# 2048 rows of the FFN's second weight in seven block products, with block sums made by DMA during the mixer

## The chip, the cores and the metric

The kernel runs on one core of one Trainium2 chip. The metric is device time in microseconds (us) of one execution. The engines that matter here are PE (TensorE, matrix products), DVE (VectorE), ACT (ScalarE), POOL (GpSimd, which is nearly idle but can issue DMAs) and SP (SyncE, which issues the DMAs of the kernel before). An engine works through its own instructions in the order in which the program lists them. An instruction whose operand isn't ready holds up all that stands behind it on that engine.

## The reference, cut to what matters

Two layers, 512 tokens, width 1024, all in float32:

```python
def swiglu(u, wi, wo):
    gate, up = jnp.split(u @ wi, 2, axis=-1)
    return (jax.nn.silu(gate) * up) @ wo          # wo: 2816 x 1024

for l in range(DEPTH):                            # DEPTH = 2
    mix = hybrid_mixer(h, ...)                    # projections, attention, recurrent branch
    h = layer_norm(ALPHA * h + mix, ...)
    h = layer_norm(ALPHA * h + cross_attention(h, mem, ...), ...)
    h = layer_norm(ALPHA * h + swiglu(h, wi[l], wo[l]), ...)
```

The change concerns the last product, `(512 x 2816) @ (2816 x 1024)`, once in each layer.

## The kernel before, in words

Every product is made to float32 accuracy out of three PE matmuls: each operand is split into a high and a low part, and high x high, high x low and low x high are added up in PSUM. So a matmul pass over a pair of 128x128 and 128x512 blocks costs three instructions.

**Weights.** The class `Weights` holds a list of pages of 128x1024 in the order of their use. `dma` has SP load a page (512 KB) into one of four buffers `raw`. `split` then makes the high half on ACT (`whi<-raw`, L122) and the low half on DVE (`wlo<-raw,whi`, L123), each into a slot of a pool of 32 pages, and starts further loads. `next` hands a page out and splits ahead as far as `la` says. The 32 slots are shared with activations and LayerNorm operands: whoever takes a slot waits until the last reader of its old tile is done.

**Matmuls.** All of them are recorded by the helper `mm` (L250), so rows are told apart by tiles. `later` and `tick` put deferred work behind so many nanoseconds of counted PE work. In `norm` each token tile's transposes (`pt`, L254) are deferred in this way: by 9500 for the first three token tiles, by 8000 for the last.

**A layer** goes through `mixer` (input projections with the attention in between, then the weights of the attention branch, the recurrent branch and gates, `w_br_rnn`, `w_out`), `cross` and `ffn`. In `ffn` the first weight is multiplied in quads (`q`, `c`: tiles of 128x256, seven block products instead of eight, with sums of weight blocks made on DVE). The hidden activations `h` stand transposed, 128 of the 2816 rows to a half page.

**The second weight** (`wo`) goes through `out_norm`: 22 pages of 128 rows. For each page and each of four token tiles there are six matmuls of 128x512 into that token tile's two PSUM banks `acc`, that is 528 matmuls per layer. The split activations are `hs` (ACT L277, DVE L278). The last pages are taken token tile by token tile, and `norm` follows each of them. The FFN's input `x`, needed as the residual, is loaded back from DRAM (`x<-x_keep`) near the end of the pages.

Of the kernel before, what the change touches and what calls it, by code (L numbers as in the profile page):

```python
# [7 lines left out]
F32 = mybir.dt.float32  # L8
F32R = mybir.dt.float32r
AF = mybir.ActivationFunctionType  # L10
ALU = mybir.AluOpType
# [3 lines left out]
P = 128  # L15
S = 512
# [25 lines left out]
def f(ap):  # L42
    return ap.bitcast(F32)


class Weights:
# [27 lines left out]
    def rows(self, w, c0, n):  # L74
        for k in range(n):
            self.specs.append([(w[k * P:(k + 1) * P, c0:c0 + D], lambda t: t)])

    def gates(self, a, b):
        for n in range(4):
            self.specs.append([  # L80
                (m[n].rearrange("(k p) c -> p k c", p=P),
                 lambda t, i=i: t[:, i * 512:(i + 1) * 512].rearrange("p (k c) -> p k c", k=2))
                for i, m in enumerate((a, b))])
# [22 lines left out]
    def split(self):  # L106
        j = self.n_split
        if j >= len(self.specs):
            return
        while self.n_dma <= j:  # L110
            self.dma()
        if j in self.quad:
            self.drain()
            self.gen = self.split_quad(j)
            self.drain()
            return
        self.n_split += 1
        nc = self.K.nc
        raw = self.raw.pop(j)
        hi = self.K.page(F32R, "whi")  # L120
        lo = self.K.page(F32R, "wlo")
        nc.scalar.activation(out=hi, in_=raw, func=AF.Copy)  # L122
        nc.vector.tensor_sub(out=lo, in0=raw, in1=f(hi))  # L123
        self.parts[j] = (hi, lo)
        while self.n_dma < min(len(self.specs), j + 1 + N_RAW):
            self.dma()

# [91 lines left out]
class Trunk:  # L219
    def __init__(self, ctx, tc, a):  # L220
        self.tc = tc
        self.nc = tc.nc
        self.a = a
        self.L = a["w_in"].shape[0]
        pool = lambda name, bufs, **kw: ctx.enter_context(tc.tile_pool(name=name, bufs=bufs, **kw))
        self.const = pool("const", 1)
        self.pg = pool("pg", N_PAGES)
        self.raw = pool("raw", N_RAW)
        self.hpool = pool("hp", 8)
        self.smp = pool("sm", 3)  # L230
        self.sml = pool("sml", 8)
        self.psp = pool("ps", 8, space=PSUM)
        self.W = Weights(self)
        self.now = 0.0
        self.pend = []

    def page(self, dt=F32, name="pg"):
# [205 lines left out]
    def norm(self, t, ps, g, b, last):  # L443
# [52 lines left out]
                                               op0=ALU.mult, op1=ALU.add)  # L496
            nc.sync.dma_start(out=self.a["out"][t * P:(t + 1) * P, c], in_=xt[:, c])
        if not last:
            self.later(9500.0 if t < NT - 1 else 8000.0, lambda: self.xT_due(t))
            if self.want_T:  # L500
                nc.sync.dma_start(out=self.x_dram[t * P:(t + 1) * P, :], in_=xt)

    def out_norm(self, act, nk, res, gv, bv, last=False, prefetch=0, between=None,
                 want_T=False, restore=False, spread=0.0):
# [6 lines left out]
        acc = [[self.ps("acc") for _ in range(2)] for _ in range(NT)]  # L511
        self.x_done = [False] * NT
        self.want_T, self.spread = want_T, spread
        self.Bf = {}

        cut = last

        def step(k, t, w, parts=((0, S), (S, D))):
            ah, al = act(k)
            hi, lo = w  # L520
            cs = slice(t * P, (t + 1) * P)
            kw = {"skip_group_check": True} if parts[0][1] - parts[0][0] < S else {}
            out = lambda c0, c1: acc[t][c0 // S][:, c0 % S:c0 % S + c1 - c0]
            for c0, c1 in parts:
                self.mm(out(c0, c1), ah[:, cs], hi[:, c0:c1], k == 0, False, **kw)
# [6 lines left out]
        for k in range(nk - res):  # L532
# [158 lines left out]
    def schedule_weights(self):  # L691
        a, W = self.a, self.W
        for l in range(self.L):
# [70 lines left out]
    def mixer(self, l, params):  # L764
# [279 lines left out]
    def ffn(self, l, last):  # L1044
        nc, a, W = self.nc, self.a, self.W
        W.la = 0
        H, hs = {}, {}

        def act(m, g, u0, u1):
            s = self.half(name="silu")  # L1050
            nc.scalar.activation(out=s, in_=g, func=AF.Silu)
            if m % 2 == 0:
                pg = self.page(F32, "h")
# [21 lines left out]
        act(1, p[2], p[3], None)  # L1075
        self.xt = [None] * NT
        for m in range(2, NF):
            act(m, *self.proj_pair())
        W.la = 2
# [28 lines left out]
    def run(self):  # L1108
        nc, a = self.nc, self.a
        self.xt = [self.page(F32, "x") for _ in range(NT)]  # L1110
        self.mT_dram = [self.tc.dram_tile([P, 2, 2, MEM], F32, name="mT_keep%d" % i) for i in range(4)]
        self.x_dram = self.tc.dram_tile([S, D], F32, name="x_keep")
        self.xT = self.const.tile([P, ND, 2, S], F32R, name="xT")
        self.ident = self.const.tile([P, P], F32, name="ident")
# [76 lines left out]
```

## Time and profile before

| what | value |
|---|---|
| median of 3 runs | 1893.18 us (1892.93 to 1893.5) |
| the profiled execution, its span | 1893.48 us, 1891.7 us |
| PE busy, TensorE clock granted | 1875.8 us (99%), 0.998 |
| DVE, ACT, POOL busy | 1360.0 us (72%), 1011.3 us (53%), 27.6 us (1%) |
| DMA moved | 217.63 MB, mean 115 GB/s |

The span is the time from the first to the last instruction. The execution is 1.78 us longer than its span. Busy time counts an engine's instructions, not its waits. PE's 99% says that nearly all of the time is time in which a matmul is under way. It doesn't say that each matmul is at its shortest.

### The profile page before, as it was taken

What the parts mean: (1) busy time and instruction counts of PE and PEld (TensorE: products, weight loads), DVE (VectorE), ACT (ScalarE), POOL (GpSimd) and SP (SyncE); (2) the same over time, 40 slices, a digit from 0 to 9 for tenths busy, and PEclk for the clock granted to TensorE, in tenths of its full rate; (3) what the DMA queues carried; (4) which work ended last, traced back from release to release, by engine and by line L of the source; (5) the groups of instructions that cost most, each with busy time, mean ns of one, the idle gap of its engine ahead of it and who ended that gap; (6) DMA issues with size and microseconds to landing.
All of it is one profiled execution on the core that took longest, in us unless ns stands there. A gap on an engine that the chain in (4) does not pass through costs nothing.

```text
span 1891.7 us, 28939 instructions
## 1 busy us (share of the span) xinstructions
PE 1875.8 (99%) x11201; PEld 1665.3 (88%) x11201; DVE 1360.0 (72%) x2435; ACT 1011.3 (53%) x1989; POOL 27.6 (1%) x74
## 2 busy tenths in 40 slices
PE   9999999999999999999999999999999999999998
PEld 8888888888998999988898888888889889999886
DVE  6997367569767888873579964675688598888634
ACT  5675167336664655652346742773367565565521
POOL 0000000000000000000000000000000000000001
PEclk9999999999999999999999999999999999999999
DMA  6434133355434333354214441333652523333531
GB/s 183 112 101 119 49 98 91 101 179 176 125 124 145 90 112 102 101 190 144 67 46 104 109 123 44 101 94 96 200 171 86 177 91 101 102 109 107 187 100 45
DMA packets 277754, 217.63 MB, mean 115 GB/s; under 512 B 7793, under 2 KB 254065, under 8 KB 277617
## 3 DMA queue, kind: packets, MB, share of 16 engines
q1 hardware_dynamic: 277616, 215.79, 38.0%
q8 instruction: 88, 1.44, 0.3%
q14 instruction: 50, 0.40, 0.1%
HBM read 196.89 MB, written 12.58 MB: 111 GB/s over the span
## 4 chain that ended last, share of the span: by engine, by line
PE 95%; DVE 3%; issue 0%; DMA 0%; ACT 0%; SPq 0%; DVEq 0%
PE ps L250 39%; PE q L250 25%; PE acc L250 22%; PE cv L250 2%; PE sc L250 2%; PE av L250 1%; PE cs L250 1%; PE pT L254 1%; PE pt L254 1%; DVE wlo L123 1%; DVE Bf L355 1%; DMA raw<-in_w_in_dram 0%; PE cT L254 0%; DVE xT L275 0%; SPq L1125 0%
## 5 line engine op out<-in xcount | busy, mean ns | idle before, releaser
L250 PE MATMUL ps<-xT,whi 128*128 128x512 f32 (+1 forms) x1728 | 478.2, 365 | 0.5 <-ACT whi L102 0.5
L123 DVE TENSOR_TENSOR wlo<-raw,whi 128x1024 fp32r<-128x1024 f32 x239 | 290.7, 1222 | 146.9 <-ACT whi L122 118.0
L250 PEld LDWEIGHTS ps<-xT,whi 128*128 128x128 f32 x1728 | 297.3, 188 | 44.2 <-ACT whi L102 0.7
L122 ACT ACTIVATE whi<-raw 128x1024 fp32r<-128x1024 f32 x239 | 249.8, 1054 | 140.3 <-PE acc L250 52.4
L250 PE MATMUL ps<-xT,wlo 128*128 128x512 f32 (+1 forms) x864 | 311.3, 362 | 0.2
L250 PE MATMUL acc<-whi,hs 128*128 128x512 f32 (+1 forms) x714 | 218.3, 387 | 0.5 <-ACT hs L277 0.5
L250 PEld LDWEIGHTS ps<-xT,wlo 128*128 128x128 f32 x864 | 162.0, 188 | 28.0 <-DVE wlo L123 0.6
L250 PEld LDWEIGHTS acc<-whi,hs 128*128 128x128 f32 x714 | 133.5, 188 | 28.0 <-ACT hs L277 0.9
L250 PE MATMUL q<-xT,wq 128*128 128x256 f32 x1152 | 154.2, 281 | 0.0
L250 PEld LDWEIGHTS q<-xT,wq 128*128 128x128 f32 x1152 | 144.1, 189 | 0.2
L409 ACT ACTIVATE c<-q 128x256 f32<-128x256 f32 x192 | 73.5, 383 | 129.9 <-PE q L250 129.3
L250 PE MATMUL acc<-wlo,hs 128*128 128x512 f32 (+1 forms) x357 | 137.9, 386 | 0.0
L275 DVE TENSOR_TENSOR wql<-s,wqh 128x512 fp32r<-128x512 f32 x192 | 129.2, 685 | 1.4 <-ACT wqh L274 1.2
L274 ACT ACTIVATE wqh<-s 128x512 fp32r<-128x512 f32 x192 | 115.0, 622 | 15.7 <-DVE s L152 14.5
L275 DVE TENSOR_TENSOR wq<-raw,wq 128x512 fp32r<-128x512 f32 x144 | 98.6, 685 | 0.0
L274 ACT ACTIVATE wq<-raw 128x512 fp32r<-128x512 f32 x144 | 89.6, 622 | 1.4 <-DMA raw<-in_cq_w_dram 1.4
L250 PE MATMUL acc<-whi,mg 128*128 128x512 f32 x256 | 80.5, 392 | 0.0
L250 PE MATMUL acc<-whi,cO 128*128 128x512 f32 x256 | 79.7, 390 | 0.0
L250 PE MATMUL ps<-ya,whi 128*128 128x512 f32 x256 | 78.8, 389 | 0.0
L250 PE MATMUL ps<-yr,whi 128*128 128x512 f32 x256 | 78.8, 389 | 0.0
L250 PEld LDWEIGHTS acc<-wlo,hs 128*128 128x128 f32 x357 | 67.0, 188 | 13.4
L250 PE MATMUL q<-T4h,wq 128*128 128x256 f32 x384 | 76.6, 282 | 0.0
(233 smaller groups left out, 3974.8 us busy)
## 6 DMA issues: line engine op xcount, KB each, us to landing
raw<-in_ffn_wi_dram SPq DMA_DIRECT2D x88, 512.0 KB, 3.8
raw<-in_w_in_dram SPq DMA_DIRECT2D x84, 512.0 KB, 3.8
raw<-in_ffn_wo_dram SPq DMA_DIRECT2D x44, 512.0 KB, 4.2
raw<-in_ckv_w_dram SPq DMA_DIRECT2D x32, 512.0 KB, 4.3
raw<-in_w_br_attn_dram SPq DMA_DIRECT2D x16, 512.0 KB, 4.1
raw<-in_w_br_rnn_dram SPq DMA_DIRECT2D x16, 512.0 KB, 4.0
raw<-in_w_out_dram SPq DMA_DIRECT2D x16, 512.0 KB, 3.7
x_keep<-x SPq DMA_DIRECT2D x16, 512.0 KB, 2.6
```

Of the source, the lines that this page charges most:

```text
L122: nc.scalar.activation(out=hi, in_=raw, func=AF.Copy)
L123: nc.vector.tensor_sub(out=lo, in0=raw, in1=f(hi))
L250: self.nc.tensor.matmul(out, lhsT=lhsT, rhs=rhs, start=start, stop=stop, **kw)
L254: self.nc.tensor.transpose(out, in_, self.ident)
L274: nc.scalar.activation(out=hi, in_=src, func=AF.Copy)
L275: nc.vector.tensor_sub(out=lo, in0=src, in1=f(hi))
L355: nc.vector.tensor_tensor(out=o, in0=x, in1=y, op=ALU.subtract)
L409: cp = lambda out, in_: nc.scalar.activation(out=out, in_=in_, func=AF.Copy)
```

## The change

For rows 0 to 2047 of `wo` (16 of the 22 pages) the product of a 512x2048 and a 2048x1024 matrix is cut 2 by 2 into blocks: tokens in halves of 256, the inner dimension in halves of 1024, the columns in halves of 512. Seven products of sums of blocks take the place of eight products of blocks. A page of a weight block holds two row blocks of 128 and 512 columns, so each product has four pages with 12 matmuls each. The last six pages go through `out_norm` as before and add to the same PSUM banks (`acc=acc, k0=16`).

- The weight's block sums B11+B12, B12+B22, B11+B12+B22 and B11+B12+B22+B21 are made in DRAM (`wsum`): ten DMAs for a group of 128 rows, eight groups per layer, all issued by POOL. Two of the ten move one element of a weight's page (`whi`) and stand first, so that the group starts when that page exists. A group is issued at every fifth split page from the end of the attention on.
- The activations' block sums (`hsum`, and in place in `h`) are made on DVE and split (`hq`) in the same way as `hs`. Two operands are made during the last two quads (`ahead`).
- Four of the seven products are added into `x` by DVE (`into_x`), so `x` is now loaded ahead of the seven products. `W.la` is 3 during them.
- In `norm` the last token tile's transposes are deferred by 9000 instead of 8000, in every `out_norm` but the last.

```diff
+    def blocks(self, w):
+        for j in range(4):
+            self.specs.append([(w[j * 256:(j + 1) * 256, :].rearrange("(k p) c -> p k c", p=P),
+                                lambda t: t.rearrange("p (k c) -> p k c", k=2))])
...
         self.parts[j] = (hi, lo)
+        self.K.block_sums(hi)
...
-            self.later(9500.0 if t < NT - 1 else 8000.0, lambda: self.xT_due(t))
+            self.later(9500.0 if t < NT - 1 else 9000.0, lambda: self.xT_due(t))
...
-            W.rows(a["ffn_wo"][l], 0, NF)
+            wo, t = a["ffn_wo"][l], self.wsum[l]
+            for b in (wo[0:D, 0:S], t[0], t[1], wo[D:2 * D, 0:S], t[2], wo[D:2 * D, S:D], t[3]):
+                W.blocks(b)
+            W.rows(wo[2 * D:DFF, :], 0, NF - 2 * ND)
+
+    def block_sums(self, page):
+        self.n_page += 1
+        if not self.bg or self.n_page % 5:
+            return
+        l, j = self.bg.pop(0)
+        dma = self.nc.gpsimd.dma_start
...
+        t1, t2, t3, t4 = (t[j * P:(j + 1) * P, :] for t in self.wsum[l])
+        for t in (t1, t3):
+            dma(out=t[0:1, 0:1], in_=f(page[0:1, 0:1]))
+        for out, in_, add in ((t1, B11, 0), (t3, B12, 0), (t1, B12, 1), (t3, B22, 1),
+                              (t2, t1, 0), (t2, B22, 1), (t4, t2, 0), (t4, B21, 1)):
+            kw = {"accum_op": ALU.add} if add else {}
+            dma(out=out, in_=in_, **kw)
...
         self.tick(flush=True)
+        self.bg = [(l, j) for j in range(8)]
...
+        W.la = 3
+        self.T = {}
+        self.xt = [self.page(F32, "x") for _ in range(NT)]
+        for t in range(NT):
+            nc.sync.dma_start(out=self.xt[t], in_=self.x_dram[t * P:(t + 1) * P, :])
+        acc = seven()
...
         W.la = 2
-        self.T = {}
         self.out_norm(h_parts, NF, R3, a["ln3_g"][l], a["ln3_b"][l], last=last,
-                      prefetch=0 if last else F3, restore=True)
+                      prefetch=0 if last else F3, acc=acc, k0=2 * ND)
...
+        def product(p, b, first):
+            for j in range(4):
+                hi, lo = (t.rearrange("p (k c) -> p k c", k=2) for t in W.next())
+                i = p * 4 + j
+                while todo and todo[0][0] * 4 + todo[0][1] <= i + 2:
+                    operand(*todo.pop(0))
+                ah, al = ops.pop((p, j))
+                for k in range(2):
+                    for t in range(2):
+                        c = slice(t * P, (t + 1) * P)
+                        self.mm(b[t], ah[:, k, c], hi[:, k, :], first and j + k == 0, False, **kw)
+                        self.mm(b[t], ah[:, k, c], lo[:, k, :], False, False, **kw)
+                        self.mm(b[t], al[:, k, c], hi[:, k, :], False, j + k == 4, **kw)
+                    self.tick()
+
+        def into_x(t0, hf, b, op):
+            for t in range(2):
+                x = self.xt[t0 + t][:, hf * S:(hf + 1) * S]
+                tt(out=x, in0=x, in1=b[t], op=op)
```

On POOL, before stood 64 small copies `sm<-sk` of the attention and nothing else until the end of the last layer. Now 80 DMAs stand behind the attention's copies of each layer. This is one group of the first layer (`wsum_0` to `wsum_3` are the four sums in DRAM, `whi` the page that it waits for, DMASW the semaphores on which POOL waits for its own earlier DMAs):

```order
L752 DMA wsum_0_86<-whi 1x1 [waits Activation_49]
L752 DMA wsum_2_88<-whi 1x1
L756 DMA wsum_0_86<-in_ffn_wo_dram 128x512 [waits DMASW6_49]
L756 DMA wsum_2_88<-in_ffn_wo_dram 128x512 [waits DMASW7_49,DMASW1_49]
L756 DMA wsum_0_86<-in_ffn_wo_dram 128x512 [waits DMASW0_49]
L756 DMA wsum_2_88<-in_ffn_wo_dram 128x512 [waits DMASW1_49]
L756 DMA wsum_1_87<-wsum_0_86 16x4096 [waits DMASW2_49]
L756 DMA wsum_1_87<-in_ffn_wo_dram 128x512 [waits DMASW5_49,DMASW4_49]
L756 DMA wsum_3_89<-wsum_1_87 16x4096 [waits DMASW5_49]
L756 DMA wsum_3_89<-in_ffn_wo_dram 128x512 [waits DMASW6_49]
```

Each of these DMAs waits for the one whose result it needs, and POOL issues nothing of the next group before the last of this one is issued.

On DVE, in the stage of the `w_br_rnn` pages of the first layer, one of the eight `wlo` now waits for POOL's DMAs too (DMASW5 and DMASW4), because it takes the slot of a page that a group's one-element DMAs read. Of the changed kernel:

```order
L922 SCALAR_TENSOR_TENSOR mg<-gate,ps 128x512 [waits PE_49]
L923 TENSOR_TENSOR mg<-mg,gate 128x512 [waits DVE_49]
L287 SCALAR_TENSOR_TENSOR mg<-mg 128x512 [waits Activation_49]
L129 TENSOR_TENSOR wlo<-raw,whi 128x1024 [waits DMASW5_49,DMAHW7_49,DMASW4_49,Activation_49]
L922 SCALAR_TENSOR_TENSOR mg<-gate,ps 128x512 [waits PE_49]
```

Each group has one such first waiter, on ACT, DVE or SP. Before, no row waits for a DMASW semaphore there.

On DVE, in the stage of the second weight of the first layer, a row pair repeated before, one `hs` and one `wlo` for 24 matmuls:

```order
L278 SCALAR_TENSOR_TENSOR hs<-h,hs 128x512 x3
L123 TENSOR_TENSOR wlo<-raw,whi 128x1024
L278 SCALAR_TENSOR_TENSOR hs<-h,hs 128x512
L123 TENSOR_TENSOR wlo<-raw,whi 128x1024
L278 SCALAR_TENSOR_TENSOR hs<-h,hs 128x512
L123 TENSOR_TENSOR wlo<-raw,whi 128x1024
```

Now operand sums (L1153, L1155) and additions into `x` (L1184) stand between them, here from the end of the first product to the end of the second, and there are 12 matmuls to a `wlo`:

```order
L1153 TENSOR_TENSOR hsum<-h 128x512 x2
L1184 TENSOR_TENSOR x<-x,acc 128x512
L287 SCALAR_TENSOR_TENSOR hq<-hsum,hq 128x512
L129 TENSOR_TENSOR wlo<-raw,whi 128x1024
L287 SCALAR_TENSOR_TENSOR hq<-hsum,hq 128x512
L1184 TENSOR_TENSOR x<-x,acc 128x512
L129 TENSOR_TENSOR wlo<-raw,whi 128x1024
L1153 TENSOR_TENSOR hsum<-h 128x512 x2
L1155 TENSOR_TENSOR hsum<-hsum,h 128x512
L287 SCALAR_TENSOR_TENSOR hq<-hsum,hq 128x512
L129 TENSOR_TENSOR wlo<-raw,whi 128x1024
```

An addition into `x` waits for the last matmul of a product, and the split pages that stand behind it wait with it.

## Rows read from the trace of the kernel before

**Rows 1.** The page: busy us of each engine, and the granted clock in 40 slices.

```profile
PE 1875.8 (99%) x11201; PEld 1665.3 (88%) x11201; DVE 1360.0 (72%) x2435; ACT 1011.3 (53%) x1989; POOL 27.6 (1%) x74
...
PEclk9999999999999999999999999999999999999999
```

**Rows 2.** The chain that ended last: start us, us, what.

```profile
172.12 220.18 PE ps L250 x957
...
626.24 198.58 PE q L250 x1668
826.50 110.50 PE acc L250 x486
...
1762.77 120.18 PE acc L250 x543
```

**Rows 3.** PE's waits: what for, us in total, times, longest us.

```profile
PE pt L254 <- DVE x L488: 2.2, 4, 0.9
PE scr L1097 <- DVE idle L1089: 1.5, 1, 1.5
PE ps L250 <- DVE wlo L123: 1.5, 2, 0.7
PE acc L250 <- ACT hs L277: 0.5, 2, 0.3
```

**Rows 4.** PE's timeline, second weight: start us, us, engine, line, what.

```profile
896.94 0.84 PE L250 MATMUL acc<-whi,hs 128*128 128x512 f32 x3
897.62 0.39 PE L250 MATMUL acc<-wlo,hs 128*128 128x512 f32 x1
897.84 0.39 PE L250 MATMUL acc<-whi,hs 128*128 128x512 f32 x1
898.07 0.39 PE L250 MATMUL acc<-wlo,hs 128*128 128x512 f32 x1
898.30 0.84 PE L250 MATMUL acc<-whi,hs 128*128 128x512 f32 x3
...
902.38 0.84 PE L250 MATMUL acc<-whi,hs 128*128 128x512 f32 x3
```

**Rows 5.** Stretches: us, busy us of each engine, granted clock, DMA share, GB/s.

```profile
626.00:826.50 200.50, 200.23 (x1683) 200.03 (x1682) 167.39 (x309) 114.22 (x237) 0.00 (x0) 1.00 0.37 111
826.50:926.00 99.50, 99.50 (x439) 82.36 (x440) 42.02 (x48) 35.07 (x44) 0.00 (x0) 1.00 0.48 151
1387.00:1425.00 38.00, 37.12 (x222) 32.95 (x222) 33.31 (x48) 23.82 (x38) 0.00 (x0) 1.00 0.67 201
215.70:445.00 229.30, 229.29 (x1035) 187.94 (x1034) 147.23 (x204) 120.89 (x179) 0.00 (x0) 1.00 0.38 117
```

**Rows 6.** DVE groups of 626 to 926 us: busy us, mean ns of one.

```profile
L123 DVE TENSOR_TENSOR wlo<-raw,whi 128x1024 fp32r<-128x1024 f32 x26 | 31.8, 1223 | 40.6 <-ACT whi L122 25.4 <-issue 8.8 <-PE acc L250 6.4
L278 DVE SCALAR_TENSOR_TENSOR hs<-h,hs 128x512 fp32r<-128x512 f32 x22 | 14.9, 686 | 11.3 <-ACT hs L277 11.3
L152 DVE TENSOR_TENSOR s<-raw 128x512 f32<-128x512 f32 x18 | 12.3, 685 | 0.0
```

**Rows 7.** DVE's timeline at the end of the quads.

```profile
809.63 0.69 DVE L275 TENSOR_TENSOR wql<-s,wqh 128x512 fp32r<-128x512 f32 x1
810.24 0.69 DVE L161 TENSOR_TENSOR s<-raw,s 128x512 f32<-128x512 f32 x1
810.84 0.69 DVE L275 TENSOR_TENSOR wql<-s,wqh 128x512 fp32r<-128x512 f32 x1
```

**Rows 8.** The page, two of ACT's groups: busy us, mean ns of one.

```profile
L122 ACT ACTIVATE whi<-raw 128x1024 fp32r<-128x1024 f32 x239 | 249.8, 1054 | 140.3 <-PE acc L250 52.4
...
L274 ACT ACTIVATE wqh<-s 128x512 fp32r<-128x512 f32 x192 | 115.0, 622 | 15.7 <-DVE s L152 14.5
```

**Rows 9.** DMA issues: engine, count, KB each, median us from issue to landing.

```profile
raw<-in_ffn_wo_dram SPq DMA_DIRECT2D x44, 512.0 KB, 4.2
x_keep<-x SPq DMA_DIRECT2D x16, 512.0 KB, 2.6
Q<-Qhl SPq DMA_DIRECT2D x48, 128.0 KB, 2.3
ln_b<-in_ln_b_dram SPq DMA_DIRECT2D x6, 512.0 KB, 8.1
raw<-in_w_rg_dram SPq DMA_DIRECT2D x8, 256.0 KB, 2.7
out_dram<-y SPq DMA_DIRECT2D x8, 256.0 KB, 2.0
```

**Rows 10.** Timeline of ACT, DVE and SP behind the first layer's attention.

```profile
174.38 1.99 ACT L122 ACTIVATE whi<-raw 128x1024 fp32r<-128x1024 f32 x2
...
368.28 1.23 DVE L123 TENSOR_TENSOR wlo<-raw,whi 128x1024 fp32r<-128x1024 f32 x1 [0.26 <-ACT whi L122]
...
392.62 0.43 SPq L508 DMA_DIRECT2D ln_g<-in_ln_g_dram  x1
```

More of the change, by code (lines that the diff above doesn't have):

```diff
@@ L234, in __init__ @@
         self.now = 0.0
+        self.bg = []
+        self.n_page = 0
         self.pend = []
@@ L503, in out_norm @@
     def out_norm(self, act, nk, res, gv, bv, last=False, prefetch=0, between=None,
-                 want_T=False, restore=False, spread=0.0):
+                 want_T=False, restore=False, spread=0.0, acc=None, k0=0):
         nc = self.nc
@@ L510, in out_norm @@
         nc.sync.dma_start(out=b, in_=bv.partition_broadcast(P))
-        acc = [[self.ps("acc") for _ in range(2)] for _ in range(NT)]
+        fresh = [[acc is None or n is None for n in row] for row in acc] if acc else [[True] * 2] * NT
+        acc = [[acc[t][i] if not fresh[t][i] else self.ps("acc") for i in range(2)] for t in range(NT)]
         self.x_done = [False] * NT
@@ L521, in step @@
             cs = slice(t * P, (t + 1) * P)
-            kw = {"skip_group_check": True} if parts[0][1] - parts[0][0] < S else {}
+            kw = {"skip_group_check": True} if k0 or parts[0][1] - parts[0][0] < S else {}
             out = lambda c0, c1: acc[t][c0 // S][:, c0 % S:c0 % S + c1 - c0]
             for c0, c1 in parts:
-                self.mm(out(c0, c1), ah[:, cs], hi[:, c0:c1], k == 0, False, **kw)
+                self.mm(out(c0, c1), ah[:, cs], hi[:, c0:c1], k == k0 and fresh[t][c0 // S], False, **kw)
                 self.mm(out(c0, c1), ah[:, cs], lo[:, c0:c1], False, False, **kw)
@@ L530, in step @@
             self.tick()
-        for k in range(nk - res):
+        for k in range(k0, nk - res):
             w = self.W.next()
@@ L723, in schedule_weights @@
                 W.quads(a["ffn_wi"][l], m * P, DFF + m * P)
-            W.rows(a["ffn_wo"][l], 0, NF)
+            wo, t = a["ffn_wo"][l], self.wsum[l]
[8 more added lines that the diff above has]
+        dma = self.nc.gpsimd.dma_start
+        wo = self.a["ffn_wo"][l]
+        B11, B12, B21, B22 = (wo[r * D + j * P:r * D + (j + 1) * P, c * S:(c + 1) * S]
+                              for r in range(2) for c in range(2))
+        t1, t2, t3, t4 = (t[j * P:(j + 1) * P, :] for t in self.wsum[l])
[5 more added lines that the diff above has]
+            dma(out=out, in_=in_, **kw)
     def layer_params(self, l):
@@ L1046, in ffn @@
         W.la = 0
-        H, hs = {}, {}
+        H, Hp, hs = {}, {}, {}
         def act(m, g, u0, u1):
@@ L1052, in act @@
             if m % 2 == 0:
-                pg = self.page(F32, "h")
+                pg = Hp[m // 2] = self.page(F32, "h")
                 H[m], H[m + 1] = pg[:, :S], pg[:, S:]
@@ L1077, in ffn @@
         for m in range(2, NF):
+            if m == NF - 2:
+                seven, ahead = self.wo_seven(Hp)
+            if m >= NF - 2:
+                ahead()
             act(m, *self.proj_pair())
+        W.la = 3
[4 more added lines that the diff above has]
+        acc = seven()
+        for m in range(2 * ND):
+            H.pop(m)
+        Hp.clear()
@@ L1079, in ffn, with wo_seven, s, operand @@
         W.la = 2
-        self.T = {}
         self.out_norm(h_parts, NF, R3, a["ln3_g"][l], a["ln3_b"][l], last=last,
-                      prefetch=0 if last else F3, restore=True)
+                      prefetch=0 if last else F3, acc=acc, k0=2 * ND)
+    def wo_seven(self, Hp):
+        nc, W = self.nc, self.W
+        tt = nc.vector.tensor_tensor
+        h = lambda j, tok: Hp[j].rearrange("p (k s) -> p k s", k=2)[:, :, tok * 256:(tok + 1) * 256]
+        st, ops = {}, {}
+        def s(j):
+            if j // 2 not in st:
+                st[j // 2] = self.page(F32, "hsum")
+            return st[j // 2][:, j % 2 * S:(j % 2 + 1) * S].rearrange("p (k s) -> p k s", k=2)
+        def operand(p, j):
+            if p in (0, 3):
+                src = h(j + (4 if p else 0), 0)
+            elif p == 6:
+                src = h(j + 4, 1)
+            elif p == 4:
+                src = h(j, 0)
+                tt(out=src, in0=src, in1=h(j, 1), op=ALU.subtract)
+            else:
+                src = s(j)
+                if p == 1:
+                    tt(out=src, in0=h(j, 1), in1=h(j + 4, 1), op=ALU.subtract)
+                elif p == 2:
+                    tt(out=src, in0=src, in1=h(j, 0), op=ALU.subtract)
+                else:
+                    tt(out=src, in0=src, in1=h(j + 4, 0), op=ALU.add)
+            t = self.page(F32R, "hq")
+            hi, lo = (t[:, i * S:(i + 1) * S].rearrange("p (k s) -> p k s", k=2) for i in range(2))
+            self.split_to(hi, lo, src, scale=1.0 / ALPHA)
+            ops[p, j] = hi, lo
+        todo = [(p, j) for p in range(7) for j in range(4)]
+        def product(p, b, first):
+            kw = {} if first else {"skip_group_check": True}
+            for j in range(4):
[15 more added lines that the diff above has]
+                tt(out=x, in0=x, in1=b[t], op=op)
+        bank = lambda: [self.ps("acc") for _ in range(2)]
+        def run():
+            b1 = bank()
+            product(0, b1, True)
+            into_x(0, 0, b1, ALU.add)
+            b2 = bank()
+            product(1, b2, True)
+            into_x(2, 1, b2, ALU.add)
+            product(2, b1, False)
+            into_x(0, 1, b1, ALU.subtract)
+            b3 = bank()
+            product(3, b3, True)
+            product(4, b1, False)
+            into_x(2, 1, b1, ALU.subtract)
+            product(5, b2, False)
+            product(6, b1, False)
+            return [[b3[0], b2[0]], [b3[1], b2[1]], [b1[0], None], [b1[1], None]]
+        return run, lambda: operand(*todo.pop(0))
@@ L1111, in run @@
         self.mT_dram = [self.tc.dram_tile([P, 2, 2, MEM], F32, name="mT_keep%d" % i) for i in range(4)]
+        self.wsum = [[self.tc.dram_tile([D, S], F32, name="wsum%d_%d" % (l, i)) for i in range(4)]
+                     for l in range(self.L)]
         self.x_dram = self.tc.dram_tile([S, D], F32, name="x_keep")
```

## The prediction

> **What bounds the kernel now.** I read the page first. PE is busy 99% of the span at full granted clock, DVE 72%, ACT 53% [rows 1]. The reader is to see two things: no clock is to be won, and hardly any idle time of PE. The chain of waits says the same in order of time. It is made of long unbroken pieces of matmuls. The second weight is the piece of 110.50 us from 826.50 in the first layer and the one of 120.18 us from 1762.77 in the second [rows 2]. The list of PE's waits holds only some 6 us, of which 2.2 us, in four places, are transposes that wait for the end of LayerNorm [rows 3].
>
> Busy 99% could hide matmuls that are slower than they need be, so I read the timeline of PE in the second weight. One record is 0.39 us long because they overlap, but the starts are what counts. From 898.30 to 902.38 there are 18 matmuls in 4.08 us, so one is issued each 0.2267 us [rows 4]. This pitch holds whichever operand is used. The kernel is bound by the number of matmuls, and fewer of them is time won, as long as what feeds them keeps up. That second half decides, so I read the stretches: in this stage DVE is busy 42.02 of 99.50 us, ACT 35.07, DMA 0.48. In the quads before it DVE is at 167.39 of 200.50 us, and PE still misses only 0.27 us [rows 5].
>
> **The change, part by part.**
>
> *Matmuls.* Sixteen pages of 24 matmuls are 384 per layer. Seven products of 4 pages with 12 each are 336. So 48 fall away per layer, 96 in all, of the same 128x512 shape. 96 x 0.2267 = **-21.8 us**. This is the only large gain. It can't be larger, since PE's pitch is fixed.
>
> *Feeding the products.* A page now lasts 12 x 0.2267 = 2.72 us of PE, where it lasted 5.44, and there are 28 of them in place of 16, so 76.2 us per layer. DVE has, per page, one `wlo` (1.22 us), one `hq` like `hs` (0.69), 16/28 of an operand sum and 8/28 of an addition into `x`, both like the 128x512 sums of the quads (0.685) [rows 6]. That is 1.22 + 0.69 + 0.39 + 0.20 = 2.50 us, 92% of 2.72. Back to back the instructions overlap (in the quads they start 0.60 us apart [rows 7]), so I expect some 2.3 us, 83%, as in the quads, where PE lost next to nothing. ACT has 1.05 + 0.62 us per page [rows 8], which is less. Loads are 512 KB per 2.72 us, 193 GB/s. The stretch with the nearest load is the cross-attention's K and V (1387 to 1425): 201 GB/s, DMA share 0.67, DVE 33.31 of 38 us. There PE is idle 0.88 us of 38, 2.3% [rows 5]. Taken over to 76.2 us this is 1.8 us per layer, **+3.5 us** for both. It also stands for the start of the second product, where DVE, in its program order, waits for the last matmul of the first before it goes on to operands that PE needs soon. Bounds: 0, as in the quads, and 9 us per layer, which is worked out with the rivals.
>
> *The loads of `x` and the additions into it.* The four loads are only moved ahead on SP; `x` is first read behind a whole product of 10.9 us, and a load of this size lands in 4.2 [rows 9]. The eight additions are in DVE's 2.50 us. PE waits for one only where a product takes its bank again, and another product of 10.9 us lies between each time. **0 us**; what they may cost as a stop on DVE is in the bound of 9.
>
> *Transposes of the last token tile, 1000 ns later.* One more us of matmuls goes ahead of them. The four waits are 2.2 us together, the longest 0.9 [rows 3], so nearly all is covered: **-2.0 us**, bounds -2.2 and 0 (the work put ahead is PE work that exists anyway).
>
> *Block sums by DMA.* They cost no engine time but POOL's issuing, and POOL has nothing else to do there. They can cost in one way: the page which starts a group is held until the group's one-element DMAs have read it. These stand on POOL behind the whole group before. The next user of that slot on ACT, DVE or SP waits, and in-order work behind it too. In the first layer the page of the first group is written at 174.4. The first waiter of the seventh group is a `wlo` that DVE ran at 368.3, that of the eighth SP's `ln_g` at 392.6 [rows 10]. If a group takes C from its first DMA to the next group's, the seventh starts at 174.4 + 6C, and PE has some 6 us more before it needs that page (it is split two pages ahead). So nothing is held while 6C < 368.3 + 6 - 174.4 = 200, C < 33 us. For `ln_g`, with 7C < 218 and about 15 us of buffered loads behind it on SP, C < 33 comes out again. The sums themselves are read only in the last quads, more than 350 us later. I take the second layer as the first.
>
> C is six dependent steps: a one-element DMA, a copy, an add, a copy, an add, a copy. No row shows a DMA issued by POOL, one from DRAM to DRAM, or one that adds, so I bound it. A write of 256 KB out landed in 2.0 us, a load of 256 KB in 2.7, a store of 512 KB in 2.6 [rows 9]. Below: 2.0 + 5 x 2.7 = 15.5 us. Above: load and store one after the other, 5.3 a step, and for the two adds another 2.7 to read the target: 2.0 + 5 x 5.3 + 2 x 2.7 = 33.9. I take about 25, near the middle, since a copy reads and writes at the same time but an add reads twice. All but the very end of these bounds costs nothing: **0 us**. At 33.9 it would be 6 x 33.9 - 200 = 3 us per layer.
>
> The Trainium skill gives a price for a DMA issued from GpSimd ("DMA: Bandwidth & Descriptors", Anatomy of one DMA): about 2.0 us fixed, mostly the receipt from the target memory, plus bytes over 436 GB/s. By this an estimate of a 256 KB step is 2.6 us and of C 15 us, and nothing would be held. [...]
>
> *Sum*, against the profiled execution: 1893.48 - 21.8 + 3.5 - 2.0 + 0 = 1873.2. That execution is 0.3 above the median of the runs, which is less than I can tell. **1873 us**, 1.1% faster.
>
> **Rivals.**
>
> *A, the products are fed too slowly.* For it speaks that DVE is at 92% by plain durations and `x` additions stop it in order. Four of them with 2 x 0.69 us are 5.5 us per layer if nothing hides them. If loads landed in 8.1 us like `ln_b` [rows 9], a `raw` buffer would be taken for 8.1 + 1.05 + 1.22 + about 1 = 11.4 us, four buffers give a page per 2.84 us, 0.12 too slow, 28 times: 3.4 us. Together 9 per layer: 1873 - 3.5 + 18 = **1888 us**. Against it: `W.la = 3` splits three pages, 8.2 us, ahead, and loads of this weight land in 4.2 us [rows 9].
>
> *B, slower: the chain of block sums is longer than the pages' pace.* This is the hold above, beyond its point. From C = 35 on, 6C - 200 = 10 us per layer eat the whole gain. If each step took 8.1 us, like the longest loads [rows 9], C is 48.6, the seventh group's page is held 92 us per layer, and the time is 1873 + 184 = **2057 us**. C = 38 gives 28 per layer, 1929 us. For it: six steps in series without overlap, of a kind that no row shows, and my upper bound reaches its threshold. Against it: it needs steps of 5.8 us on average with 256 KB or less, where 512 KB loads land in 4.2.
>
> *C, the block sums slow the weight loads.* A group writes 8 x 256 KB, 2.1 MB in some 27 us, 77 GB/s next to the 117 GB/s and the DMA share of 0.38 of that stretch [rows 5]. In proportion the share becomes 0.63, or 0.88 if reading counts again. A page there lasts 5.44 us, so four buffers bear 4 x 5.44 - 3.3 = 18 us of landing time. Loads would have to become four times as slow; at 20 us a page takes (20 + 3.3) / 4 = 5.8 us, and 45 pages lose 17 us per layer: **1907 us**. The Trainium skill speaks for this rival ("DMA: Bandwidth & Descriptors", Issuing engines are not separate DMA queues): DMAs issued by GpSimd run on the same 16 engines and interleave with SP's. No row here shows two issuers at once; the K and V stretch shows only that a share of 0.67 of one queue is borne.
>
> **How the numbers follow.** My forecast 0.70, with its own range 1869 (no stall, all 2.2 us of the transposes won) to 1880 (twice the stalls, no gain from the transposes, a few held us). A 0.12, its slower half at or near no change, B 0.15, C 0.03. A measurement of this kernel can tell about 0.2%, 3.8 us. Faster: 0.70 + 0.06 = 0.76, same 0.06, slower 0.15 + 0.03 = 0.18. The range takes the forecast and A: 1868 to 1891, and leaves B and C out.
>
> **What would show it.** The second weight's piece of the chain about 11 us shorter in each layer, with matmuls still 0.227 apart. PE's waits for `wlo` or `hq` some 1 to 2 us per layer at the first and second product. The `pt` waits gone. Between 174 and 420 us and in the same stretch of the second layer, PE without gaps, and POOL's DMAs landing in about 4 us each with groups some 27 us apart. I'm wrong if ACT, DVE or SP wait there for POOL's DMAs, if landing times of `raw` pass 18 us, or if PE's waits in the products add up to more than 5 us per layer.

## The result, and the profile after

The change takes the median from 1893.33 us (1892.93 to 1893.5, 4 runs) to **1870.34 us** (1869.67 to 1870.37, 4 runs). The ratio is 0.9877, with a 95% interval of 0.9863 to 0.9892. The profiled execution of the changed kernel took 1869.67 us, its span is 1867.9 us. I had forecast 1873 us, in a range of 1868 to 1891.

The page of the changed kernel, busy us of each engine and the granted clock, answers to [rows 1]:

```profile
PE 1855.3 (99%) x11105; PEld 1648.1 (88%) x11105; DVE 1428.0 (76%) x2531; ACT 1045.7 (56%) x2037; POOL 129.9 (7%) x234
...
PEclk9999999999999999999999999999999999999999
```

PE has 96 matmuls less and is 20.5 us less busy; DVE has 68 us more to do. PE's share stays at 99%, which alone would not tell the two kernels apart.

The chain of the changed kernel in order of time (start us, us, what), at the same places as [rows 2], with the second weight's pieces at 825.19 and 1749.83:

```profile
171.75 220.20 PE ps L259 x957
...
825.19 99.84 PE acc L259 x438
925.91 5.47 PE acc L259 x24
...
1098.65 220.19 PE ps L259 x957
...
1749.83 109.56 PE acc L259 x495
```

And two more pieces of the chain of the kernel before:

```profile
937.87 5.47 PE acc L250 x24
...
1110.59 220.20 PE ps L250 x957
```

The pieces of the quads can't be compared by their starts, since they hold 1668 matmuls before and 1678 after. So these places are taken from PE's timeline, at a matmul that has the same number of matmuls ahead of it in both kernels: the first one that reads `T1h`, an operand of the quads, and the first of the second weight. In the first layer, of the kernel before and then of the change:

```profile
627.50 0.28 PE L250 MATMUL q<-T1h,wqh 128*128 128x256 f32 x1
...
826.50 0.50 PE L250 MATMUL acc<-whi,hs 128*128 128x512 f32 x1 [0.27 <-ACT hs L277]
```

```profile
626.44 0.28 PE L259 MATMUL q<-T1h,wqh 128*128 128x256 f32 x1
...
825.03 0.40 PE L259 MATMUL acc<-whi,hq 128*128 128x512 f32 x1
```

Read side by side, the starts give the gain stage by stage:

| place | before | after | gained since the place above |
|---|---|---|---|
| end of the first attention | 172.12 | 171.75 | 0.37 |
| quads of the first FFN, first `T1h` | 627.50 | 626.44 | 0.69 |
| second weight's first matmul | 826.50 | 825.03 | 0.41 |
| its last pages | 937.87 | 925.91 | 10.49 |
| second layer, behind the attention | 1110.59 | 1098.65 | -0.02 |
| quads of the second FFN, first `T1h` | 1563.77 | 1551.06 | 0.77 |
| second weight's first matmul | 1762.77 | 1749.66 | 0.40 |
| end of the span | 1891.7 | 1867.9 | 10.69 |

So 21.2 of 23.8 us come from the stage of the second weight, 1.5 from the transition into the FFN, 0.8 from the transition into the second weight, and 0.4 from the start of the program. The last is no effect of the change: in the runs below in which nothing delays it, the same piece begins anywhere from 171.70 to 172.34. The stretch that holds most of the block sums, from 172 to 392 us and again from 1099 us, is as long as before, 220.20 us.

PE's waits in the changed kernel answer to [rows 3]; neither `pt` nor `acc` stands among them now:

```profile
PE ps L259 <- DVE wlo L129: 1.8, 4, 0.7
PE scr L1220 <- DVE idle L1212: 1.5, 1, 1.5
PE ps L259 <- ACT whi L108: 0.4, 1, 0.4
```

The stretches of the seven products (all of them in the first layer, then an inner one) and the stretch behind the attention, with the columns of [rows 5]:

```profile
825.20:901.50 76.30, 76.30 (x335) 62.50 (x335) 69.91 (x88) 47.85 (x62) 0.00 (x0) 1.00 0.73 244
...
836.00:847.00 11.00, 11.00 (x48) 8.45 (x47) 11.00 (x15) 4.52 (x6) 0.00 (x0) 1.00 0.43 144
...
215.00:445.00 230.00, 229.99 (x1040) 188.61 (x1039) 147.89 (x207) 121.05 (x180) 40.27 (x62) 1.00 0.66 175
```

DVE is busy 69.91 of 76.30 us and in an inner stretch without any pause, 11.00 of 11.00. DVE is near its limit here, and one of the runs below shows how near. PE's busy time misses nothing, but it hides something: the 48 matmuls of the second product take 11.40 us in the first layer and 11.41 in the second, where 48 x 0.2267 are 10.88. PE's loads of the stationary operand, which have an engine row of their own (PEld), do wait there (us in total, times, longest):

```profile
PEld acc L259 <- DVE hq L287: 1.0, 4, 0.3
PEld acc L259 <- ACT hq L286: 0.7, 2, 0.4
```

DVE's largest group in the same stretch (x count | busy us, mean ns | idle before):

```profile
L129 DVE TENSOR_TENSOR wlo<-raw,whi 128x1024 fp32r<-128x1024 f32 x33 | 40.1, 1219 | 3.2 <-PE acc L259 2.1 <-ACT whi L128 1.1
```

In the last row of the stretches DMA works at a share of 0.66 in place of 0.38, and PE misses nothing either.

One group of block sums on POOL in the first layer, start us, us, what, with what ended the wait before it in brackets:

```profile
320.20 1.07 POOL L752 DMA_DIRECT2D wsum<-whi  x2 [2.48 <-ACT whi L128]
324.13 1.08 POOL L756 DMA_DIRECT2D wsum<-in_ffn_wo_dram  x2 [2.85 <-DMA wsum<-whi]
329.14 1.69 POOL L756 DMA_DIRECT2D wsum<-in_ffn_wo_dram  x2 [3.94 <-DMA wsum<-in_ffn_wo_dram]
335.71 0.52 POOL L756 DMA_DIRECT2D wsum<-wsum  x1 [4.87 <-DMA wsum<-in_ffn_wo_dram]
341.13 0.82 POOL L756 DMA_DIRECT2D wsum<-in_ffn_wo_dram  x1 [4.90 <-DMA wsum<-wsum]
346.16 0.52 POOL L756 DMA_DIRECT2D wsum<-wsum  x1 [4.21 <-DMA wsum<-in_ffn_wo_dram]
...
349.83 1.32 POOL L752 DMA_DIRECT2D wsum<-whi  x2
...
380.41 1.31 POOL L752 DMA_DIRECT2D wsum<-whi  x2
```

The group begins when its page is there (ACT `whi` ended the wait), takes six dependent steps, and 29.6 us later the next begins, without a wait for its page: from here on in this layer the chain sets the pace, not the pages. The next one, the eighth and last, follows 30.6 us later, and its own last DMA is issued 35.3 us after its first (415.73). In the second layer the chain sets the pace four times, with 27.2, 25.3, 27.0 and 29.9 us, and the last group takes 35.6. The order on POOL is not quite the one told ahead of the prediction: in the first layer the second group's one-element DMAs go out at 193.47, ahead of the first group's last steps, and the two groups run into each other. The landing times (KB each, median us), and what loads next to them paid:

```profile
wsum<-in_ffn_wo_dram POOLq DMA_DIRECT2D x96, 256.0 KB, 4.8
...
wsum<-wsum POOLq DMA_DIRECT2D x32, 256.0 KB, 3.6
raw<-in_w_br_rnn_dram SPq DMA_DIRECT2D x16, 512.0 KB, 6.1
...
wsum<-whi POOLq DMA_DIRECT2D x32, 0.0 KB, 3.5
```

The medians for one element, 3.5 us, and for a copy of 256 KB within DRAM, 3.6, lie close together, but they hide a wide spread. Ten of the 32 one-element DMAs landed in 1.5 to 1.6 us. The other 22 took 2.9 to 7.5, and 18 of these went out while the last add of the group before was still under way. The copies of 256 KB took 2.8 us at least. How much of a step's time goes with its bytes is not shown, since no run changed them.

### The profile page after: what moved, and what is told of

Read it like the earlier page. It is cut to its first block, busy times and chain, and to the rows that moved or that the text cites. A ratio compares the mean times of both kernels' runs of the same rounds, so it can differ in the third digit from the quotient of the medians.

```text
span 1867.9 us, 29249 instructions
## 1 busy us (share of the span) xinstructions
PE 1855.3 (99%) x11105; PEld 1648.1 (88%) x11105; DVE 1428.0 (76%) x2531; ACT 1045.7 (56%) x2037; POOL 129.9 (7%) x234
## 3 DMA queue, kind: packets, MB, share of 16 engines
q0 software_dynamic: 13824, 33.57, 8.8%
## 4 chain that ended last, share of the span: by engine, by line
PE 97%; DVE 2%; ACT 0%; issue 0%; DVEq 0%
PE ps L259 41%; PE q L259 26%; PE acc L259 21%; PE cv L259 2%; PE sc L259 2%; PE av L259 1%; PE cs L259 1%; PE pt L263 1%; PE pT L263 1%; DVE wlo L129 1%; PE cT L263 0%; DVE Bf L364 0%; DVE xT L284 0%; PE scr L1220 0%; DVE cK L284 0%
## 5 line engine op out<-in xcount | busy, mean ns | idle before, releaser
L129 DVE TENSOR_TENSOR wlo<-raw,whi 128x1024 fp32r<-128x1024 f32 x263 | 319.3, 1220 | 91.1 <-ACT whi L128 87.9
L128 ACT ACTIVATE whi<-raw 128x1024 fp32r<-128x1024 f32 x263 | 274.9, 1053 | 99.5 <-DMA raw<-in_w_out_dram 17.1
L259 PE MATMUL acc<-whi,hq 128*128 128x512 f32 x448 | 139.2, 391 | 0.0
L283 ACT ACTIVATE wqh<-s 128x512 fp32r<-128x512 f32 x192 | 115.0, 622 | 15.7 <-DVE s L159 15.5
L259 PEld LDWEIGHTS acc<-whi,hq 128*128 128x128 f32 x448 | 83.8, 188 | 18.9 <-DVE hq L287 1.0
L259 PE MATMUL acc<-wlo,hq 128*128 128x512 f32 x224 | 87.2, 389 | 0.0
L756 POOL DMA_DIRECT2D wsum<-in_ffn_wo_dram x96 | 70.2, 761 | 211.7 <-DMA wsum<-wsum 110.4
```

What stands on the lines that cost most here:

```text
L259: self.nc.tensor.matmul(out, lhsT=lhsT, rhs=rhs, start=start, stop=stop, **kw)
L283: nc.scalar.activation(out=hi, in_=src, func=AF.Copy)
L756: dma(out=out, in_=in_, **kw)
```

## The experiments

My theory: the time is matmuls times pitch, everything added hides below PE, and it stands on two things, DVE's rate in the products and the pace of the block sums' chain. The rivals: the added traffic costs something after all (so the gain could be larger without it); the hold of pages is harmless; the deeper split-ahead `W.la = 3` is what feeds the products.

### Is anything of the block sums paid for? (no_sums)

```diff
-        self.bg = [(l, j) for j in range(8)]
...
-            for b in (wo[0:D, 0:S], t[0], t[1], wo[D:2 * D, 0:S], t[2], wo[D:2 * D, S:D], t[3]):
+            for b in (wo[0:D, 0:S], wo[0:D, S:D], wo[D:2 * D, 0:S], wo[D:2 * D, 0:S], wo[0:D, S:D],
+                      wo[D:2 * D, S:D], wo[0:D, 0:S]):
```

> The changed kernel without any of the 160 block-sum DMAs: where a product should read a sum of two or more blocks of the weight, it reads one block of the weight, so the output is another one; matmuls, splits and loads are the same in number and shape. If the block sums are hidden completely (my theory), 1870.3 within 0.7 us. If their traffic or the held pages cost something that the profile does not show as a wait, it is faster by 1 us or more, and the two stretches of 220 us behind the attention become shorter.

Measured: **1870.47 us** (1870.11 to 1870.58), against 1870.34 with the sums. The stretch behind the first attention, in the run without sums, with the columns as above:

```profile
171.75:392.00 220.25, 220.25 (x960) 179.80 (x959) 128.92 (x155) 105.89 (x142) 0.00 (x0) 1.00 0.32 93
```

DMA works at half the share there, 0.32 in place of 0.65 with the sums, and PE's time is the same. So the 160 DMAs and 33.57 MB cost nothing that this comparison can tell, as they are placed.

### The transposes (last_8000, before_9000)

```diff
-            self.later(9500.0 if t < NT - 1 else 9000.0, lambda: self.xT_due(t))
+            self.later(9500.0 if t < NT - 1 else 8000.0, lambda: self.xT_due(t))
```

> The changed kernel with the last token tile's transposes deferred by 8000 again. By the two traces the later transposes gave back 0.47 us at each of the two transitions from cross-attention to FFN: 1870.3 + 0.9 = 1871.3 us, with PE's waits for x (L488's line) back at 0.9 us twice. By the sum of the prediction (2.0 us at four places): 1872.3.

Measured: **1871.61 us** (1871.08 to 1872.31), 1.3 us above the change. The wait is back in the list:

```profile
PE pt L263 <- DVE x L497: 2.2, 4, 0.9
```

The kernel before with 9000 alone:

> The kernel before with only the transposes deferred by 9000 in place of 8000. 1893.3 - 0.9 = 1892.4 us if the gain is 0.47 us at two places, 1891.3 if it is the 2.0 us of the prediction, 1893.3 if the wait only moves.

Measured: **1892.13 us** (1891.87 to 1892.38, 10 runs), where the kernel before has 1893.06 beside it (1892.81 to 1893.46, 13 runs): 0.9 us, with a ratio of 0.9995 (0.9985 to 1.0004) whose interval includes no change. So this edit alone stays within what the interval can tell; the two pairs of medians give 1.3 and 0.9 us, both less than the sum's 2.0. PE's timeline says what became of the rest. Its matmuls from the third token tile's transposes to the last one's (window, us, PE busy and its matmuls in brackets, then the columns of [rows 5]), and these transposes, of the kernel before and then of the change:

```profile
603.00:610.98 7.98, 7.08 (x62) 6.90 (x60) 7.98 (x19) 5.45 (x12) 0.00 (x0) 1.00 0.01 2
...
610.98 1.06 PE L254 MATMUL pt<-ident,x 128*128 128x128 f32 x8 [0.90 <-DVE x L488]
```

```profile
602.64:610.61 7.97, 7.90 (x69) 7.72 (x67) 7.97 (x19) 5.45 (x12) 0.00 (x0) 1.00 0.01 2
...
610.61 1.06 PE L263 MATMUL pt<-ident,x 128*128 128x128 f32 x8
```

The transposes begin as late as before (0.37 us earlier, the offset of the whole program), because the LayerNorm that they wait for ends when it did. Seven more matmuls of 0.12 us now run ahead of them, 0.83 us; 0.13 of it is lost again right behind them, and 0.70 us is won. The second layer wins the same, and so does each layer in the trace of before_9000. That is 1.4 us, at two of the four places; at the others it was 0.2 us waits that moved to the next `wlo`. The 0.47 us in the two expectations come from the starts of the quads' pieces in the chain, which are not at the same matmul in the two kernels.

### What feeds the products? (la_2, la_1, no_ahead, dve_twice)

```diff
-        W.la = 3
+        W.la = 2
```

> The changed kernel with pages split two ahead instead of three during the seven products. DVE is busy 11.0 of 11.0 us in four stretches of the products, so I expect the third page to be what covers its backlog: with two ahead PE waits for wlo or hq some 1 to 4 us per layer, 1872 to 1878 us. If DVE's plain average (2.50 us of work per 2.72 us page) were all that counts, two pages ahead do as well: 1870.3.

Measured: **1869.67 us** (1869.01 to 1869.95). My expectation failed: the third page covers nothing. So I went further, to `W.la = 1`:

> The changed kernel with pages split only one ahead during the seven products. la_2 cost nothing, so the third page isn't what covers DVE's full stretches. If one page ahead (2.72 us) still covers a page's 2.3 to 2.5 us on DVE behind an addition into x (two of 0.69 us), 1870.3; if an addition that waits for the end of a product then stops the split that PE needs next, 1 to 2.5 us at each of the four additions, 4 to 10 us per layer, 1878 to 1890 us.

Measured: **1869.29 us** (1869.10 to 1869.54), the fastest of all, 1.05 us below the change, with ranges that don't touch though the two were not timed side by side; ratio to before 0.9873 (0.9858 to 0.9887). In its trace the 48 matmuls of the second product take 10.88 us in both layers, 0.5 less than in the change, and no load of PE's stationary operand waits for `hq`. DVE's timeline at the end of the first product shows the difference, first of the change, then of la_1:

```profile
835.46 0.69 DVE L1184 TENSOR_TENSOR x<-x,acc 128x512 f32<-128x512 f32 x1 [2.48 <-PE acc L259]
836.06 0.69 DVE L287 SCALAR_TENSOR_TENSOR hq<-hsum,hq 128x512 fp32r<-128x512 f32 x1
```

```profile
830.97 0.69 DVE L287 SCALAR_TENSOR_TENSOR hq<-hsum,hq 128x512 fp32r<-128x512 f32 x1 [0.16 <-ACT hq L286]
...
835.64 1.37 DVE L1184 TENSOR_TENSOR x<-x,acc 128x512 f32<-128x512 f32 x2 [1.51 <-PE acc L259]
```

In the change, the first operand of the second product is split behind the addition that waits for the first product's end, when PE wants it at once. From 836.84 on, three matmuls take 0.94 us there where they take 0.84 otherwise; with three more such places up to 843 us, where the next operand is late too, this makes up most of the 0.5 us. In la_1 fewer pages stand in front of that operand, and it is ready 5 us earlier.

The operands made ahead of the products are another matter:

```diff
         for m in range(2, NF):
...
-            if m >= NF - 2:
-                ahead()
             act(m, *self.proj_pair())
```

> The changed kernel without the two operands made during the last two quads. The first product then begins with its first operand's split behind the last quad on ACT and DVE (0.63 and 0.69 us), and before the change the first matmul of the second weight waited 0.27 us for the same thing. 1 to 3 us per layer: 1872 to 1876 us, with PE waiting for hq or wlo at the start. If ACT and DVE have enough room there: 1870.8 (the 0.48 us of the trace, half of it each layer, or all).

Measured: **1879.61 us** (1877.63 to 1883.63), +9 us, more than I expected. PE's timeline and ACT's at the start of the products, in this run:

```profile
827.51 0.62 PE L259 MATMUL acc<-whi,hq 128*128 128x512 f32 x1 [2.22 <-ACT hq L286]
827.93 0.63 PE L259 MATMUL acc<-wlo,hq 128*128 128x512 f32 x1
829.04 1.22 PE L259 MATMUL acc<-whi,hq 128*128 128x512 f32 x2 [0.48 <-DVE hq L287]
```

```profile
824.95 1.99 ACT L128 ACTIVATE whi<-raw 128x1024 fp32r<-128x1024 f32 x2
826.85 1.66 ACT L286 ACTIVATE hq<-h 128x512 fp32r<-128x512 f32 x3
```

The first `hq` now stands behind two `whi` on ACT, which PE didn't need first. That is 2.2 us of waiting and 0.5 for DVE. But matched matmul by matmul the first layer is 4.5 us behind the change eight matmuls later, and still 4.0 at the end of the stage: the second product loses nothing in this run, which gives 0.5 back. So some 1.7 us are left beyond the two waits, and they fall in the stretch of a lower clock. A stretch behind the wait:

```profile
830.00:831.00 1.00, 1.00 (x4) 0.74 (x3) 1.00 (x2) 0.91 (x1) 0.00 (x0) 0.50 0.89 297
```

After PE had stood idle for 2.2 us, the granted clock was 0.50, the lower of its two levels (1.2 GHz), for some 3 us, and the matmuls came 0.42 us apart, not 0.227.

How near is DVE to its limit?

```diff
             self.split_to(hi, lo, src, scale=1.0 / ALPHA)
+            nc.vector.scalar_tensor_tensor(out=lo, in0=src, scalar=1.0 / ALPHA, in1=f(hi),
+                                           op0=ALU.mult, op1=ALU.subtract)
```

> The changed kernel with the low half of each of the 28 operands per layer made twice on DVE, the same value both times: 28 more instructions of 128x512, 0.60 us each when back to back, 16.8 us per layer. DVE was busy 69.91 of 76.30 us in the products, so it would have 86.7 us of work for 76.3. If DVE becomes the bound, as rival A has it, the products get 4 to 10 us longer per layer (10.4 less what is split ahead): 1878 to 1891 us, with PE waiting for wlo or hq. If its busy time overstates what it can't take on, since records overlap, less than 4 us in all.

Measured: **1887.51 us** (1885.71 to 1891.32), +17.2 us, 8.6 per layer in the mean. PE's waits and the first layer's products in this run:

```profile
PE acc L259 <- DVE hq L1161: 7.3, 9, 1.6
```

```profile
825.20:911.00 85.80, 81.92 (x345) 64.80 (x345) 83.62 (x112) 45.96 (x60) 0.00 (x0) 0.98 0.61 201
```

The products now end near 909, DVE is busy 83.62 of 85.80 us up to 911, and it is DVE that PE waits for. So rival A's mechanism is real. In the change some 8% of the stretch are left to DVE, and part of what fills it is work for the pages that follow.

### The pace of the chain (steps_8, every_3, every_4, no_touch)

```diff
         for out, in_, add in ((t1, B11, 0), (t3, B12, 0), (t1, B12, 1), (t3, B22, 1),
-                              (t2, t1, 0), (t2, B22, 1), (t4, t2, 0), (t4, B21, 1)):
+                              (t2, t1, 0), (t2, B22, 1), (t2, t1, 0), (t2, B22, 1), (t4, t2, 0), (t4, B21, 1)):
```

> The changed kernel with two more dependent steps in each group: the copy and the add that make t2 are done a second time, with the same result. Groups took 29.6, 30.6 and 35.3 us where the chain set their pace, about 5 us a step, so now some 40. If a group's page is held until the group before is done (rival B of the prediction as a mechanism), the seventh group's page frees near 396 us where its next user ran at 368, the eighth's near 438 where SP's ln_g was at 392: 24 to 34 us of PE waits per layer, 1918 to 1938 us. If only the traffic counts, no more than 1872.

Measured: **1930.58 us** (1930.26 and 1930.9), ratio to before 1.0197 (1.0177 to 1.0218): 60 us above the change, by the trace 24 in the first layer and 35 in the second. Who waited for the one-element DMAs, on DVE, SP and ACT (us in total, times, longest):

```profile
DVE wlo L129 <- DMA wsum<-whi: 34.2, 3, 16.9
...
SPq L517 <- DMA wsum<-whi: 17.9, 1, 17.9
...
ACT mg L286 <- DMA wsum<-whi: 29.2, 2, 15.4
```

The first two are waiters that the prediction named: a `wlo` among the `w_br_rnn` pages, and SP's `ln_g` (L517). POOL's starts of the fourth to the eighth group stand at 271.13, 307.86, 343.00, 376.96 and 414.32, so a group takes 34 to 37 us. Two more steps of 256 KB made a kernel that gains 1.2% into one that loses 2%.

The group sums as they are, but started more often (`% 5` becomes `% 3` or `% 4` in `block_sums`):

> The changed kernel with a group at every third page in place of every fifth, the groups themselves unchanged. Pages that start a group come each 16 us then, the chain of a group takes about 28, so groups run behind and hold pages longer. By the slots in the program the sixth and seventh group's pages are wanted at about 293 and 317 us, and their one-element DMAs are reached at about 303 and 333: 5 to 20 us of waits per layer, 1880 to 1910 us. If the pace of the starts doesn't matter as long as the sums are ready by 820 us: 1870.3.

> The changed kernel with a group at every fourth page. Pages that start a group come each 22 us, the chain of a group took 24 to 31 us when it ran by itself (26.4 us between starts in every_3), so a group runs some 4 us later than its page for each group before it, 25 us by the seventh. If the hold decides, a few waits where slots are wanted early: 0 to 8 us per layer, 1870 to 1886 us, between every_3 and the change. If every fifth is needed for something else than the hold, no prediction of the size.

Measured: every third page **1896.70 us** (1894.01 to 1903.02, 8 runs), ratio 1.0021 (1.001 to 1.0033), slower than before; every fourth **1870.02 us** (1869.72 to 1870.25), as the change. With every third page:

```profile
DVE wlo L129 <- DMA wsum<-whi: 24.9, 2, 12.8
```

With every fourth the trace still has one such wait, 7.0 us on ACT, but it doesn't reach PE:

```profile
ACT mg L286 <- DMA wsum<-whi: 7.0, 1, 7.0
```

The DMAs are the same in all three. What differs is how far the groups run behind their pages, and which later slot that holds.

Without the one-element DMAs:

```diff
-        for t in (t1, t3):
-            dma(out=t[0:1, 0:1], in_=f(page[0:1, 0:1]))
```

> The changed kernel without the one-element DMAs, so that nothing holds a group back. The program's order on POOL then has the groups at its very start, and the attention's first six copies sm<-sk stand behind 26 of the DMAs, the others behind six to eight each. The copies were needed from 22 us on, each 4 us. At about 4 us a dependent step they come at 70 us and later, and the attention waits for them: slower by 50 to 200 us, 1920 to 2070 us. If the order on POOL doesn't matter, since these copies are small, 1870.3.

Measured: **1951.30 us** (1948.98 and 1953.62), ratio 1.0307 (1.0286 to 1.0327): 81 us above the change. POOL's first copies of the attention in this run:

```profile
47.60 2.16 POOL L647 COPY sm<-sk 128x2 f32<-128x2 f32 x6
97.30 0.20 POOL L647 COPY sm<-sk 128x2 f32<-128x2 f32 x1
```

The six copies ran at 47.60 where before they ran at 21.88, and the next not until 97.30, where before it ran at 49.67. PE came to the end of the attention 78 us late (the piece of 220.20 us begins at 249.72). So the hold keeps the sums off POOL's queue during the attention. That they need it for nothing else was not tested.

## Why the prediction was right, step by step

- **Matmuls, -21.8 us.** Right. The stage gained 10.49 and 10.69 us, 21.2 together, with the loss of the next point in it, and outside that place the pitch is 0.2267 still.
- **Feeding the products, +3.5 us.** It was +1.0. The mechanism that I named for it, the start of the second product, is there and is nearly all of it: 0.5 us in each layer, which la_1 takes away. Mis-sized was the transfer of 2.3% of idle time from the K and V stretch [rows 5]. Of that stretch's 0.88 us, 0.74 is a single wait for a `wlo`, at 1393.59, not a loss that goes with the load's rate. DVE's measured share of 91.6% (69.91 of 76.30 us) looks like the 92% of my plain sum, but that is chance. DVE's durations in the stretch add up to 76.4 us and overlap to 69.91, as my discount had it, and it does more than the 28 pages there. With 33 `wlo` and three `hs` it already splits for the pages that follow, and my sum left these out. By starts 1.13 us apart for a `wlo` and 0.60 for the others, an estimate for the products alone is 63 us or 82%.
- **Additions into `x`, 0 us.** Right in the total. `x` loads landed later than I had it, 7.8 us in the median of the three landings on the trace, still ahead of use: the first addition, at 835.46, waited for PE.
- **Transposes, -2.0 us.** About -1.4 by the traces, 0.9 to 1.3 by the medians. The step took nearly the whole of all four waits as covered by 1000 ns of deferral; seven matmuls, 0.83 us, went ahead at two places, and the other two waits moved to the next operand.
- **Missed: about -1 us.** The two operands made during the last quads take away the wait for the first `hs`, which stands in [rows 3] with 0.5 us in two places. The second weight's first matmul comes 0.41 and 0.40 us earlier by it, and the next few, which stood up to 0.34 us apart before, another 0.1 each. I listed the wait and did not count it. no_ahead shows that without these operands 9 us of the gain are lost.
- **The sum.** 1873.2 against 1869.67 for the profiled execution is 3.5 us off: 2.5 from feeding, 1.0 from the missed wait, 0.4 from the start of the program and 0.2 behind the last matmul, less 0.6 from the transposes.
- **Block sums, 0 us.** Right, with less room than I thought. I took C as 25 in bounds of 15.5 and 33.9; where the chain set the pace it was 25 to 31, and the last group of each layer took 35 us to its last DMA, which holds no page any more. The Trainium skill has a price for such a DMA ("DMA: Bandwidth & Descriptors", Anatomy of one DMA): about 2.0 us fixed, and bytes over 436 GB/s on top; an estimate by it is 2.6 us for 256 KB and 15 us for C. Here the quickest landings, 1.5 us for one element and 2.8 for 256 KB, are near that price; the medians of 3.5, 3.6 and 4.8 us, next to the other DMAs, are not, so the measurement decides.
- **Rival B** did not happen but is real, and its formula gives the right order only: at C of 34 to 37, 6C - 200 gives 4 to 22 us per layer, and steps_8 lost 24 and 35. It holds no term for the waits of ACT (29.2 us) and behind `ln_g` (17.9), it takes the second layer as the first, and it leaves out the lower clock (0.985 in the mean in that run).
- **Rival A.** Its mechanism is shown by dve_twice. My reason against it, that `W.la = 3` splits three pages ahead, was wrong: one page ahead feeds the products as well. What keeps A away is that DVE's work per page is below PE's: 16.8 us more of it per layer made PE wait.
- **Rival C** is shown not to be so at this rate: loads of `w_br_rnn` landed in 6.1 us in place of 4.0, those of `w_in` in 4.8 in place of 3.8, far from 18, and no_sums is no faster. The Trainium skill says ("DMA: Bandwidth & Descriptors", Issuing engines are not separate DMA queues) that DMAs of different issuers run on the same engines. These slower loads agree with it; it was no reason to expect a loss.

## What to carry to other kernels

Where PE is bound by its number of matmuls, work taken off it is won one for one, and everything that replaces it is to be added up on each other engine, with what that engine makes for the next stage in the same time. Where PE's busy time shows no gap, the starts of its matmuls and the waits of its operand loads can still show one. A DMA that reads a page holds the page's slot until it has run, so a chain of dependent DMAs on a queue must be about as short as the pace of the pages that start it, or its lag grows with each group until a page is wanted; count its steps. Where an operand is first needed behind another stage, see what stands ahead of it on its engine, and make it earlier.

## What the runs showed that I had not expected

- PE paid twice for a long wait: after 2.2 us of waiting in no_ahead the granted clock was 0.50 for some 3 us, and about 1.7 us were lost there beyond the waits in each layer. Before the transposes, a wait of 0.90 us had no such effect.
- Two streams of DMA at a share of 0.66 made loads of 512 KB a quarter to a half slower, and cost nothing. That the four buffers cover it was not tested by itself.
- A chain of 25 to 31 us on a page pace of 27 is harmless for eight groups and one of 34 to 37 costs 60 us; started at every third page the same 160 DMAs cost 26 us. Between harmless and slower than before lie two steps per group.
